# Dilated attention of a two-layer decoder: blocks spread over more steps, negated scores, combinations on two engines, x norms through the weight ring

## The chip, the cores and the metric

The kernel runs on one core of a Trainium2 chip. The metric is the time of one execution on the device in microseconds (us), and lower is better. A core has TensorE (PE; its weight loads are shown as PEld), VectorE (DVE), ScalarE (ACT), GpSimd (POOL) and a queue, SyncE (SP), from which this kernel issues its transfers between DRAM and the on-chip memory (SBUF). Results of matrix products land in PSUM, here eight banks of 128 x 512 words. Each engine works through its own list of instructions in order; semaphores tie the lists together.

## The reference

One sequence of 2048 tokens of width 1024 passes two layers, in float32. Layer 0 is an mLSTM mixer (four heads, a recurrent matrix memory with a running maximum), layer 1 is causal attention with three groups of four heads, which all read the same keys and values. Group `g` sees 128 keys back at a distance of 1, 4 or 16 tokens. After each mixer a gated embedding is added.

```python
def dilated_layer(h, k, v, norm_g, w_in, qnorm_g, w_out, cos, sin):
    proj = rms_norm(h, norm_g) @ w_in
    q, z = jnp.split(proj, [B_QW], axis=-1)
    q = apply_rope(rms_norm(q, qnorm_g), cos, sin)       # 3 groups x 4 heads x 128
    for g, (window, dilation) in enumerate(((128, 1), (512, 4), (2048, 16))):
        o_g, l_g = dilated_window_attention(q[:, :, g], k, v, window, dilation)
        ...
    wts = jax.nn.softmax(jnp.stack(lses, axis=0), axis=0)
    o = jnp.einsum('gbsh,gbshd->bshd', wts, jnp.stack(outs, axis=0))
    return (o.reshape(...) * jax.nn.silu(z)) @ w_out

for layer in range(2):
    h = h + (mlstm_layer(...) if layer == 0 else dilated_layer(...))
    h = h + (p[layer] @ w_ple[layer]) * jax.nn.sigmoid(rms_norm(h) @ w_ple_gate[layer])
```

## The kernel before

**Products.** Tokens are worked in four groups `g` of 512 (four tiles of 128). Each float32 operand is split into a rounded high part and the rest (`wh`, `wl`; `xh`, `xl`), and three products are added in PSUM. `project` (L150) runs a projection: per step of 128 rows of the weights it loads `wraw` on SP, splits it on ScalarE (`wh`, L102) and VectorE (`wl`, L104 or L106), and issues 12 products of 128 x 512 (L167 or L169). `wraw`, `wh` and `wl` are rings of five buffers each. Loads are written with a higher priority, so that the scheduler puts them ahead.

**Side work.** After each step `project` calls `pump()`, which advances the first generator of the list `side` by one step. So the steps of the mLSTM, and later of the attention, are laid between projections. `staged(units)` starts one attention unit per call and advances those that live. A unit (`attend`) is one block of 128 queries: loads `kr`, `qr`, `vt`; transposes to `kT`, `qT` (L664, copies L666); scores (L695); mask and row maximum in one VectorE operation into `pr` and `md` (L701); the negated maximum `nm` (L704); `exp` on ScalarE with the sum (L707); transposes of `pr` (L715, copies L719); products with the values (L726); then `finish`. For groups 1 and 2 `finish` is `spill`: the output on ScalarE (L734) and the statistics on VectorE (L735) go to `ot`, and from there to `o1d` or `o2d` in DRAM (L736). For group 0 it is `combine`: it loads the other two groups' rows to `oo`, forms weights from the three statistics, and adds the three outputs (L776, L778) into `y`, which POOL multiplies with `z` (L780). `held_back` does this later for the four tiles of the first token group. `turn` transposes finished `y` (L182) for the output projection.

**Stages.** For each `g`: `a_in` (projections of layer 0; `norms(g + 1)` reads the next x into `xraw`, L318, and squares it), `a_out` (`mix_out`, then `ple(0, g)`), and `b_in`, which projects keys (`w_kv`), values, queries and `z`. `normrope` normalises and rotates on the way to DRAM: L594 and L600 on VectorE, L601 to L605 on POOL. Its tables `tab` are made on POOL from `cst` (L571, L576 to L578), a load per table. The blocks of group 1 start after `a_out` of the last `g`; group 2 and the rest start in `b_in(3)` after its `queries(2)`. What is left of the list runs afterwards with no products beside it, up to the transposes of `y`; then `mix_out` and `ple` of layer 1 follow for each `g`, with group 0's blocks of the next ones between their steps.

## Time and profile before

| | us |
|---|---|
| median of 3 runs | 2351.04 |
| lowest and highest run | 2348.55, 2352.8 |
| profiled execution, its own time | 2347.66 |
| span of its trace | 2345.8 |
| TensorE busy | 2313.6 |
| VectorE busy | 1543.6 |
| ScalarE busy | 1128.3 |
| POOL busy | 593.0 |

The granted clock of TensorE in the profiled execution is 0.997 of full speed. TensorE's share of the span is 99%; the rows of the engines below it overlap with it and with each other. A row of the waits names the waiting engine, its line and what it waited for; a row of the timeline gives a start, a duration, the engine and line, what is written from what, and in brackets the idle time ahead of it with what ended it.

### The profile page before, as it was taken

How to read it: one execution, taken by the hardware profiler on the slowest of the kernel's cores; microseconds unless marked ns; L12 is line 12 of the kernel's file. 1: busy time of each engine (PE TensorE's matmuls, PEld its weight loads, DVE VectorE, ACT ScalarE, POOL GpSimd, SP SyncE). 2: the span in 40 equal slices, each digit the busy share in tenths (PEclk: the TensorE clock that was granted, in tenths of full speed). 3: DMA queues.
4: the chain of work that ended last, by engine and by line, in shares of the span. 5: the costliest groups of instructions: out<-in, count | busy, mean ns of one | idle time of the engine just before them, and what ended most of it. 6: DMA issues, size and time to landing. Idle time of an engine off the chain costs nothing.

```text
span 2345.8 us, 35374 instructions
## 1 busy us (share of the span) xinstructions
PE 2313.6 (99%) x11760; PEld 1977.5 (84%) x11760; DVE 1543.6 (66%) x3405; ACT 1128.3 (48%) x2731; POOL 593.0 (25%) x719
## 2 busy tenths in 40 slices
PE   9999999999999999999999999999999998999999
PEld 7889888888888888889888888888898887888887
DVE  6846665776566667747575675566755668786866
ACT  5434454543344545434444543344664666453643
POOL 5011235601211644011225601212202121220301
PEclk9999999999999999999999999999999999999999
DMA  5433344533244455333344543253674777465453
GB/s 184 125 91 115 99 149 162 183 116 121 61 123 125 146 164 165 117 91 111 103 130 142 174 125 120 64 171 117 203 221 134 231 237 228 135 198 164 145 160 98
DMA packets 190246, 337.14 MB, mean 144 GB/s; under 512 B 21552, under 2 KB 38256, under 8 KB 190064
## 3 DMA queue, kind: packets, MB, share of 16 engines
q1 hardware_dynamic: 189920, 334.86, 46.1%
q8 instruction: 93, 1.52, 0.3%
q14 instruction: 89, 0.73, 0.1%
q10 hardware_dynamic: 144, 0.02, 0.0%
HBM read 284.27 MB, written 50.53 MB: 143 GB/s over the span
## 4 chain that ended last, share of the span: by engine, by line
PE 85%; DVE 6%; DMA 4%; POOL 2%; ACT 2%; issue 1%; SPq 0%; ACTq 0%; DVEq 0%; POOLq 0%
PE bank L169 41%; PE bank L167 32%; PE bank L726 2%; PE bank L695 2%; PE bank L664 1%; DVE wl L104 1%; PE bank L525 1%; PE bank L526 1%; PE bank L528 1%; PE bank L715 1%; PE bank L182 1%; DMA oo<-o2d 1%; PE bank L512 1%; DMA o2d<-ot 1%; DVE xl L106 1%
## 5 line engine op out<-in xcount | busy, mean ns | idle before, releaser
L169 PE MATMUL bank<-wh,xh 128*128 128x512 f32 (+1 forms) x1664 | 642.5, 386 | 2.8 <-ACT wh L102 2.8
L169 PE MATMUL bank<-wl,xh 128*128 128x512 f32 (+1 forms) x1664 | 622.0, 374 | 0.8 <-DVE wl L104 0.8
L169 PE MATMUL bank<-wh,xl 128*128 128x512 f32 (+1 forms) x1664 | 622.6, 374 | 0.0
L102 ACT ACTIVATE wh<-wraw 128x512 fp32r<-128x512 f32 (+1 forms) x544 | 326.7, 603 | 549.5 <-PE bank L167 302.8
L104 DVE TENSOR_TENSOR wl<-wraw,wh 128x512 fp32r<-128x512 f32 (+1 forms) x512 | 353.9, 695 | 318.7 <-ACT wh L102 317.3
L167 PE MATMUL bank<-xh,wh 128*128 128x512 f32 x1272 | 501.9, 395 | 0.4 <-ACT xh L102 0.4
L167 PE MATMUL bank<-xh,wl 128*128 128x512 f32 x1272 | 496.0, 390 | 0.0
L167 PE MATMUL bank<-xl,wh 128*128 128x512 f32 x1272 | 495.9, 390 | 0.0
L169 PEld LDWEIGHTS bank<-wh,xh 128*128 128x128 f32 x1664 | 313.9, 189 | 51.0 <-ACT wh L102 3.1
L169 PEld LDWEIGHTS bank<-wh,xl 128*128 128x128 f32 x1664 | 313.4, 188 | 50.3
L169 PEld LDWEIGHTS bank<-wl,xh 128*128 128x128 f32 x1664 | 314.2, 189 | 49.3 <-DVE wl L104 1.2
L206 POOL TENSOR_TENSOR acc<-acc,sq 128x512 f32<-128x512 f32 x105 | 162.1, 1545 | 546.7 <-ACT sq L205 543.8
L167 PEld LDWEIGHTS bank<-xl,wh 128*128 128x128 f32 x1272 | 239.1, 188 | 50.5
L167 PEld LDWEIGHTS bank<-xh,wh 128*128 128x128 f32 x1272 | 239.4, 188 | 48.3 <-ACT xh L102 0.6
L167 PEld LDWEIGHTS bank<-xh,wl 128*128 128x128 f32 x1272 | 239.6, 188 | 47.8
L106 DVE SCALAR_TENSOR_TENSOR wl<-wraw,gam,wh 128x512 fp32r<-128x512 f32 x192 | 159.8, 833 | 154.1 <-ACT wh L102 151.5
L102 ACT ACTIVATE wh<-wraw,gam 128x512 fp32r<-128x512 f32 x192 | 138.0, 721 | 195.2 <-PE bank L169 134.8
L707 ACT ACTIVATE pr<-pr,nm 128x256 f32<-128x256 f32 (+1 forms) x192 | 86.6, 453 | 43.5 <-DVE nm L704 43.3
L601 POOL TENSOR_SCALAR ssb<-ssb,r 128x4 f32<-128x4 f32 x64 | 27.3, 426 | 254.1 <-ACT jk L194 233.0
L695 PE MATMUL bank<-kT,qT 128*128 128x128 f32 x600 | 78.5, 278 | 7.0 <-DVE pT L719 2.9
L695 PEld LDWEIGHTS bank<-kT,qT 128*128 128x128 f32 x600 | 72.8, 192 | 10.5 <-DVE pT L719 4.5
L726 PEld LDWEIGHTS bank<-vt,pT 128*128 128x128 f32 x600 | 75.3, 194 | 3.9
(413 smaller groups left out, 2957.4 us busy)
## 6 DMA issues: line engine op xcount, KB each, us to landing
wraw<-in_w_pg SPq DMA_DIRECT2D x128, 256.0 KB, 2.8
wraw<-in_w_in_b SPq DMA_DIRECT2D x128, 256.0 KB, 2.8
wraw<-in_w_z SPq DMA_DIRECT2D x96, 172.0 KB, 2.3
wraw<-in_w_v SPq DMA_DIRECT2D x64, 256.0 KB, 2.6
wraw<-in_w_o SPq DMA_DIRECT2D x64, 256.0 KB, 2.7
wraw<-in_w_out_a SPq DMA_DIRECT2D x64, 256.0 KB, 2.6
wraw<-in_w_kv SPq DMA_DIRECT2D x64, 256.0 KB, 2.7
kr<-kd SPq DMA_DIRECT2D x53, 256.0 KB, 4.2
```

The costliest lines, as they stand in the source:

```text
L102: nc.scalar.mul(dst_h, src, scale)
L104: nc.vector.tensor_tensor(dst_l, src, dst_h.bitcast(F32), op=ALU.subtract)
L106: nc.vector.scalar_tensor_tensor(dst_l, src, scale, dst_h.bitcast(F32), op0=ALU.mult, op1=ALU.subtract)
L167: nc.tensor.matmul(acc[i], w[:, cs], x, start=first, stop=last)
L169: nc.tensor.matmul(acc[i][:, :n], x[:, cs], w, start=first, stop=last)
L182: nc.tensor.transpose(tp[:, t * P:(t + 1) * P], tiles[t][:, k * P:(k + 1) * P], ident)
L206: eng.tensor_tensor(acc, acc, sq, op=ALU.add)
L512: nc.tensor.matmul(sp[:, h * P:(h + 1) * P], qk[:, NH + h, ts_], qk[:, h, ts_], start=True, stop=True)
L601: nc.gpsimd.tensor_scalar(ss, ss, r2[:, t:t + 1], EPS, op0=ALU.mult, op1=ALU.add)
L695: nc.tensor.matmul(sp[:, hh * n + j * P:hh * n + (j + 1) * P], qT[:, hs], kvs[j]["k"][:, hs], start=True, stop=True)
L707: nc.scalar.activation(pr[:, hh, :n], pr[:, hh, :n], AF.Exp, bias=nm[:, h:h + 1], accum_out=md[:, 4 + h:5 + h])
L726: nc.tensor.matmul(op[:, hs], pTs[h // 2][:, c0 + j * P:c0 + (j + 1) * P], kvs[j]["v"][:, hs], start=j == 0, stop=j == nk - 1)
```

## The change

The change has seven parts.

1. `norms(g + 1)`: the loads of x use the ring `wraw`, one per step of the first `w_o` projection, instead of their own `xraw`.
2. Rope tables: four loads `cst` in four buffers serve both tables of a token group (before, one load per table in two buffers). `b_in` projects `queries(2)` first, then keys, values, the other queries and `z`.
3. `normrope`: the addition `ob + tt` moves from VectorE to POOL.
4. `attend`: queries are scaled by a negative number, masks are positive, the row minimum is taken, and `exp` uses a scale of -1 with `md` as its bias, so `nm` is gone. A unit with one key block uses one bank, one `pr` and one `pT` for its four heads. The statistics are written straight into `ot`, which has two buffers.
5. The combination: per tile, two wide POOL multiplications and two wide VectorE additions replace eight small VectorE operations; the two maxima and the sums become reductions. `held_back` loads three steps later.
6. The order of units: the first sixteen (group 1's blocks 0 to 2, group 0's first four) start after `mix_out` of the last `g`, one every two steps (`GAP`); after `queries` of `b_in(3)` come group 2, the combinations of the first tiles, group 0's next four and group 1's last block.
7. `ple(1, 0)`'s 48 products with `w_p` run ahead of layer 1 with attention steps between, and their results are kept (`early`). The unhidden steps `EX` are gone. `WARM` is 20 instead of 24.

```diff
+GAP = 1
-WARM = 24
+WARM = 20
     def norms(g):
-        sq = new_acc()
-        for k in range(KD):
-            raw = wp.tile([P, T], F32, name="xraw", tag="xraw", bufs=2)
-            nc.sync.dma_start(raw, I["xT"][g, k])
-            squares(sq, k, raw)
+        def one(k):
+            with tc.high_priority(offset=PRE // 2):
+                raw = raw_piece(I["xT"][g, k], T)
+                ...
+                squares(sq[0], k, raw)
...
-            acc = project(I["w_o"][grp], 512, 8, X, False)
+            acc = project(I["w_o"][grp], 512, 8, X, False, hooks={} if grp else nsq)
...
-        cst = sm.tile([P, P], F32, name="cst", tag="cst", bufs=2)
+        cst = sm.tile([P, P], F32, name="cst", tag="cst", bufs=NT)
...
-            nc.vector.tensor_tensor(ob, ob, tt, op=ALU.add)
+            nc.gpsimd.tensor_tensor(ob, ob, tt, op=ALU.add)
...
+        queries(2, {5: lambda: st.update(r=token_rstd(sq))})
+        tabk = [rope_table(c, 0) for c in csts]
+        acc = project(I["w_kv"][0], 512, 8, X, False, gam[:, G_KV])
...
-        queries(2)
         late()
         queries(1)
...
                 nc.vector.tensor_tensor_reduce(
-                    out=pr[:, hh, :n], in0=sp[:, hh * n:(hh + 1) * n], in1=mk,
-                    scale=1.0, scalar=-3.0e38, op0=ALU.add, op1=ALU.max, accum_out=md[:, h:h + 1])
-            nc.vector.tensor_scalar_mul(nm[:, h0:h0 + 2], md[:, h0:h0 + 2], -1.0)
...
+                    out=pr[:, cs], in0=sp[:, cs], in1=mk,
+                    scale=1.0, scalar=3.0e38, op0=ALU.add, op1=ALU.min, accum_out=md[:, h:h + 1])
+                nc.scalar.activation(pr[:, cs], pr[:, cs], AF.Exp, scale=-1.0, bias=md[:, h:h + 1],
+                                     accum_out=md[:, 4 + h:5 + h])
...
     def spill(od, r, res, b):
-        def go(op, md):
-            ot = bp.tile([P, 520], F32, name="ot", tag="ot", bufs=1)
-            nc.scalar.copy(ot[:, 0:512], op)
-            nc.vector.tensor_copy(ot[:, 512:], md)
+        def begin():
+            ot = bp.tile([P, 520], F32, name="ot", tag="ot", bufs=2)
+            return ot, ot[:, 0:8]
+        def go(op, ot):
+            nc.scalar.copy(ot[:, 8:520], op)
             nc.sync.dma_start(strided(od, r, res, b, 0, 520), ot)
...
-                nc.scalar.mul(y[:, hs], op[:, hs], ee[:, 0, h:h + 1])
-                for j in range(2):
-                    nc.vector.scalar_tensor_tensor(
-                        y[:, hs], oo[:, j, hs], ee[:, 1 + j, h:h + 1], y[:, hs], op0=ALU.mult, op1=ALU.add)
+        for j in range(2):
+            o3 = oo[:, 520 * j + 8:520 * j + 520].rearrange("p (h c) -> p h c", h=NH)
+            nc.gpsimd.tensor_tensor(o3, o3, ee[:, j].unsqueeze(2).broadcast_to([P, NH, P]), op=ALU.mult)
+        for h in range(NH):
+            nc.scalar.mul(y[:, hs], op[:, hs], ee[:, 2, h:h + 1])
+        for j in range(2):
+            nc.vector.tensor_tensor(y, y, oo[:, 520 * j + 8:520 * j + 520], op=ALU.add)
...
+    def begin():
+        nonlocal bp
+        pa.close()
+        bp = ctx.enter_context(tc.tile_pool(name="bp", bufs=2))
+        side.append(staged(group1(range(3), {}) + group0(0, True), GAP))
+    X, sq = a_out(NG - 1, *a_in(NG - 1), begin)
+    b_in(NG - 1, X, sq, lambda: side.append(staged(
+        group2() + combined(0) + group0(1, False) + group1((3,), {}))))
...
+    early = {}
+    pT = embedded(1, 0)
+    for grp in range(2):
+        acc = project(I["w_p"][1, grp], 512, 2, pT, True, 0.5)
+        early[grp] = [pj() if grp == 0 else bp.tile([P, 512], F32, name="ep", tag="ep", bufs=NT) for _ in acc]
+        ...
+                nc.scalar.copy(e, a)
-    for _ in range(EX):
-        pump()
```

The scheduler sets the order of each engine's list. Three places follow; the line numbers of the changed kernel are its own. The first is SP near the start of the kernel, while group 0's `w_k` and `w_z` are loaded. Before:

```order
L571 DMA cst<-in_cs 128x128 x2
L111 DMA wraw<-in_w_z 128x344
L571 DMA cst<-in_cs 128x128 x2
L111 DMA wraw<-in_w_z 128x344
L318 DMA xraw<-in_xT 128x512 x2
L571 DMA cst<-in_cs 128x128 x2
L111 DMA wraw<-in_w_z 128x344
L318 DMA xraw<-in_xT 128x512 x2
```

And in the changed kernel, at the same place:

```order
L586 DMA cst<-in_cs 128x128
L110 DMA wraw<-in_w_k 128x512 x4
L586 DMA cst<-in_cs 128x128
L110 DMA wraw<-in_w_k 128x512
L586 DMA cst<-in_cs 128x128 x4
L110 DMA wraw<-in_w_k 128x512
L586 DMA cst<-in_cs 128x128 x2
L110 DMA wraw<-in_w_z 128x344 x8
```

The `cst` loads moved ahead of `w_z`, whose eight loads stand together; the `xraw` loads are gone from here.

The second place is ScalarE in the middle of group 2's units, under the projections of `b_in(3)`. Numbers behind a name tell one buffer's use from the next. Before:

```order
L734 COPY ot_18741<-bank_18736 128x512
L719 COPY pT_18753<-bank_18750 128x256
L666 COPY kT_18780<-bank_18775 128x512
L707 ACTIVATE pr_18760,md_18755<-pr_18760,nm_18756 128x128 x2
L707 ACTIVATE pr_18769,md_18755<-pr_18769,nm_18756 128x128 x2
L102 ACTIVATE wh_19270<-wraw_19268,gam_86 128x512
L734 COPY ot_18818<-bank_18813 128x512
```

In the changed kernel `ot_18595`, `ot_18662` and `ot_18729` belong to three units in a row:

```order
L755 COPY ot_18595<-bank_18715 128x512
L689 COPY kT_18749<-bank_18744 128x512
L727 ACTIVATE pr_18735,ot_18729<-pr_18735,ot_18729 128x128 x2
L101 ACTIVATE wh_19185<-wraw_19183,gam_86 128x512
L727 ACTIVATE pr_18735,ot_18729<-pr_18735,ot_18729 128x128 x2
L755 COPY ot_18662<-bank_18782 128x512
```

The output copy of a unit now stands behind the four `exp` of the unit after it, one `pT` copy is gone, and the `exp` write into `ot`.

The third place is TensorE near the end of the attention, in the steps before the first transposes of `y`. Before:

```order
L664 MATMUL bank_20191<-ident_75,kr_20163 128x128 x4
L664 MATMUL bank_20198<-ident_75,qr_20165 128x128 x4
L715 MATMUL bank_20211<-ident_75,pr_20174 128x128 x4
L715 MATMUL bank_20218<-ident_75,pr_20185 128x128 x2
L695 MATMUL bank_20227<-kT_20143,qT_20203 128x128
```

In the changed kernel, where `xh_19622` and `wh_19992` are p and `w_p` of layer 1:

```order
L687 MATMUL bank_19959<-ident_75,kr_19853 128x128 x4
L687 MATMUL bank_19966<-ident_75,qr_19855 128x128 x4
L166 MATMUL bank_19867<-xh_19622,wh_19992 128x512
L687 MATMUL bank_19973<-ident_75,kr_19857 128x128 x4
L166 MATMUL bank_19867<-xh_19622,wl_19993 128x512
```

The products of the embedding, which stood in `ple(1, 0)`, now lie between the transposes of the last units.

More of the change, by code (lines that the diff above doesn't have):

```diff
@@ L33 @@
 W0 = 4
-NL = 2
-EX = 3
+GAP = 1
 HO = {0: (6,), 1: (7, 2), 2: (3,), 3: (4,), 4: (5,)}
@@ L313, in norms, with first @@
     def norms(g):
-        sq = new_acc()
-        for k in range(KD):
-            raw = wp.tile([P, T], F32, name="xraw", tag="xraw", bufs=2)
-            nc.sync.dma_start(raw, I["xT"][g, k])
-            squares(sq, k, raw)
-        ahead[g] = st = {}
-        return rstd_hooks(st, sq, N1, N2, "rba")
+        sq = []
+        def one(k):
+            with tc.high_priority(offset=PRE // 2):
+                raw = raw_piece(I["xT"][g, k], T)
+                if not sq:
+                    sq.append(new_acc())
+                squares(sq[0], k, raw)
+        ahead[g] = st = {}
+        def first():
+            st["r"] = token_rstd(sq[0])
+            st["d"] = spread(st["r"])
+        return {k: lambda k=k: one(k) for k in range(KD)}, {
+            N1: first, N2: lambda: st.update(rb=row_rstd(st["d"], "rba"))}
     def a_in(g):
@@ L605, in normrope @@
             nc.gpsimd.tensor_tensor(o3, o3, rq.unsqueeze(2).broadcast_to([P, NH, P]), op=ALU.mult)
             nc.sync.dma_start(dst, ob)
-        tabk = [rope_table(g, t, 0) for t in range(NT)]
-        st = {}
-        acc = project(I["w_kv"][0], 512, 8, X, False, gam[:, G_KV], hooks={5: lambda: st.update(r=token_rstd(sq))})
-        rst = st["r"]
-        half = sm.tile([P, NT], F32, name="halfb", tag="halfb", bufs=2)
-        nc.vector.tensor_scalar_mul(half, rst, 0.5)
-        r2 = sm.tile([P, NT], F32, name="r2", tag="r2", bufs=2)
@@ L615, in b_in, with queries @@
-        nc.vector.scalar_tensor_tensor(r2, rst, 1.0 / P, rst, op0=ALU.mult, op1=ALU.mult)
+        csts = [angles(g, t) for t in range(NT)]
+        tabs = [rope_table(c, 1) for c in csts]
+        def queries(grp, hooks={}):
+            acc = project(I["w_in_b"][grp], 512, 8, X, False, gam[:, G_B], hooks=hooks)
+            if hooks:
+                settle()
+            with tc.high_priority(offset=EVAC):
+                for t in range(NT):
+                    normrope(acc[t], t, 1, -P ** -0.5, qd[rows(t), grp * 512:(grp + 1) * 512], tabs[t])
@@ L624, in b_in @@
                 nc.sync.dma_start(vd[rows(t), :], b)
-        tabs = [rope_table(g, t, 1) for t in range(NT)]
-        def queries(grp):
-            acc = project(I["w_in_b"][grp], 512, 8, X, False, gam[:, G_B])
-            with tc.high_priority(offset=EVAC):
-                for t in range(NT):
-                    normrope(acc[t], t, 1, P ** -0.5, qd[rows(t), grp * 512:(grp + 1) * 512], tabs[t])
-        queries(2)
         late()
@@ L784, in keep, with combine @@
+    def combine(n):
+        return lambda: stats("md"), lambda op, md: mix(n, *loads(n), op, md)
     def keep(y, held):
@@ L787, in go, with staged @@
             held.append(md)
-        return go
+        return lambda: stats("md0"), go
     def held_back(n, y, held):
-        _, loads, mix = combine(n, y)
-        t = loads()
         yield
-        mix(*t, y, held[0])
         yield
-    def staged(units):
+        yield
+        t = loads(n)
+        yield
+        mix(n, *t, y, held[0], y)
+        yield
+    def staged(units, gap=0):
         live = []
@@ L810, in staged @@
             yield
+            for _ in range(gap):
+                yield
     def group1(blocks, kvs):
@@ L844, in turn @@
         transposed(ys[g], (k,), None, X)
+    early = {}
[3 more added lines that the diff above has]
+        early[grp] = [pj() if grp == 0 else bp.tile([P, 512], F32, name="ep", tag="ep", bufs=NT) for _ in acc]
+        with tc.high_priority(offset=EVAC):
+            for e, a in zip(early[grp], acc):
+                nc.scalar.copy(e, a)
     Y = {}
     while len(done0) < NT:
-        pump()
-    for _ in range(EX):
         pump()
```

165 lines of the change are left out of this document (82 added, 83 removed).

## The prediction

> **What bounds the kernel now.** I read the page first, then the waits of TensorE over the whole trace, then its busy time by stretch, and last the places where it waits.
>
> ```profile
> span 2345.8 us, 35374 instructions
> PE 2313.6 (99%) x11760; PEld 1977.5 (84%) x11760; DVE 1543.6 (66%) x3405; ACT 1128.3 (48%) x2731; POOL 593.0 (25%) x719
> ```
>
> TensorE works for 2313.6 of 2345.8 us. The change keeps all its products but four warm-ups, so it can win only TensorE's 32.2 us of idle time and what hangs on it. It takes 336 instructions from VectorE, which is no gain by itself. The waits say where the idle time is (columns: us in total, times, longest).
>
> ```profile
> PE bank L715 <- ACT pr L707: 4.1, 5, 2.0
> PE bank L664 <- DMA qr<-qd: 3.5, 1, 3.5
> PE bank L695 <- DVE pT L719: 2.9, 3, 1.2
> PE bank L169 <- ACT wh L102: 2.8, 1, 2.8
> PE bank L664 <- DMA kr<-kd: 2.5, 1, 2.5
> PE bank L462 <- DVE ga L452: 1.8, 1, 1.8
> PE bank L695 <- ACT xh L102: 1.7, 1, 1.7
> PE bank L169 <- DVE wl L104: 0.8, 1, 0.8
> 52.00:90.00 38.00, 32.53 (x163) 28.99 (x162) 34.45 (x74) 16.39 (x34) 7.25 (x13) 0.91 0.46 131
> 90.00:1640.00 1550.00, 1549.87 (x7413) 1314.44 (x7412) 990.42 (x1931) 702.39 (x1615) 435.74 (x532) 1.00 0.41 126
> 1805.00:1905.00 100.00, 96.91 (x658) 87.08 (x657) 65.67 (x254) 67.38 (x249) 22.38 (x32) 1.00 0.69 220
> 1926.00:1963.00 37.00, 28.29 (x203) 24.70 (x202) 30.83 (x127) 24.96 (x72) 5.63 (x4) 0.95 0.85 269
> ```
>
> In the windows the first numbers are the stretch and TensorE's busy time, then weight loads, VectorE, ScalarE, POOL, the granted clock, and the DMA share. From 90 to 1640 us TensorE is full: whatever the change does there is worth nothing unless it opens a gap. The idle time stands near the start (5.5 us in 52 to 90) and in the attention from 1640 on.
>
> **The change part by part: the start.** In before, SP stands at the rope-table loads and the `xraw` loads with the `w_z` weights behind them.
>
> ```profile
> SPq L571 <- POOL tab L577: 15.8, 8, 3.1
> 29.17 0.52 POOL L576 TENSOR_TENSOR tab<-qkg,cst 128x64 f32<-128x64 f32 x1 [2.57 <-DMA cst<-in_cs]
> 53.92 0.38 SPq L111 DMA_DIRECT2D wraw<-in_w_z  x1
> 54.51 0.32 PE L169 MATMUL bank<-wl,xh 128*128 128x344 f32 x1
> 54.67 0.32 PE L169 MATMUL bank<-wh,xl 128*128 128x344 f32 x1
> 57.81 0.66 PE L169 MATMUL bank<-wh,xh 128*128 128x344 f32 x1 [2.83 <-ACT wh L102]
> 60.05 0.49 PE L169 MATMUL bank<-wh,xh 128*128 128x344 f32 x1
> 60.34 0.49 PE L169 MATMUL bank<-wl,xh 128*128 128x344 f32 x1
> 1.42 5.38 PE L75 MATMUL bank<-onesr 128*128 128x128 f32 x24 [1.42 <-DVE onesr L64]
> ```
>
> SP waits 15.8 us in eight places for POOL's tables, 2.0 each. A weight goes out at 53.92, and the products that want it could have started at 54.83 and have to wait, 2.8 + 0.8 us. After that products start 0.29 us apart (60.05, 60.34) instead of 0.16 (54.51, 54.67), for some 16 products until about 64 us: another 2.1 us, and the row of 52 to 90 has a granted clock of 0.91. In the changed order four `cst` buffers serve both tables, `xraw` is gone from here, and all eight `w_z` loads stand together before the `w_v` loads. POOL's eight tables, begun at 29.17 and 2.0 us each, then end by about 46 us, and the first `w_z` product is due at about 53. I take the 3.6 and the 2.1 as won, and 1.4 of the 1.8 at `ga`, which waits for VectorE's backlog. If the tables stay in the way, nothing is won. Four warm-ups fewer are worth between 0 and 4 x 0.22 = 0.9 (5.38 / 24 each), since the first product also waits for its weights; I take 0.35. Start: -7.45 (range 0 to -8.7).
>
> **Norms through the weight ring.** 24 loads of x move from the start of `w_z` into the first `w_o` projection, in the ring with the weights. SP carries one load more per step of 12 products (2.7 us at the 0.23 from start to start shown below), and ScalarE one square. The cover is the full stretch 90 to 1640; I cost it at 0. If a slot came back late, each of 24 steps could lose some tenths, at most 5 us in all.
>
> **The first units of attention.** Before, twelve block units start after `w_q` of the last group and wait 1.7 us for `xh`. Now `staged` with a gap of one starts them under the embedding stage, one unit every two steps, 44 steps in all. TensorE has 24 products per unit there. I win 1 us of the old wait and charge 1.5 for attention at three projection changes that had none (0 to 5, the 2.9 us at L695 above being what three such changes cost before). Sum +0.5.
>
> **Queries before keys.** Group 2's first unit reads `qd` just after the store.
>
> ```profile
> 1796.04 0.32 SPq L606 DMA_DIRECT2D qd<-pj  x1
> 1801.13 0.88 PE L664 MATMUL bank<-ident,qr 128*128 128x128 f32 x4 [3.50 <-DMA qr<-qd]
> 1802.66 0.63 PE L169 MATMUL bank<-wh,xl 128*128 128x512 f32 x1
> 1805.24 0.39 PE L169 MATMUL bank<-wh,xh 128*128 128x512 f32 x1
> 1805.47 0.40 PE L169 MATMUL bank<-wl,xh 128*128 128x512 f32 x1
> ```
>
> TensorE waits 3.5 us, then some eight products run 0.63 long until a later one takes 0.39 again, starting 0.23 apart (1805.24, 1805.47): 0.2 more for each, 1.7. Now `queries(2)` comes three projections before its first reader. -5.2 (0 to -5.2; what is late next is `kd`, whose last store lies a projection back).
>
> **Minimum of negated scores, statistics in `ot`.** 96 `nm` operations and 32 `ot<-md` copies leave VectorE; of the 4.1 us that TensorE waited for `pr` I take 0.9 as won (0 to 2), since an `exp` now follows its `ISA` without `nm`. But the first `ISA` of a unit now writes `ot`, which has two buffers, so it waits for the store of the unit two before. That store follows the `ot` copy on ScalarE, which stands behind the four `exp` of the unit between. This closes a loop once per unit. (Units with one key block also copy `pT` once on VectorE, instead of half on each engine; the transposes stay the same, and I cost that at 0, since VectorE is busy 3.15 of 6.00 us in the row of 1864 below.)
>
> ```profile
> 1864.39 0.58 ACT L734 COPY ot<-bank 128x512 f32<-128x512 f32 x1 [0.21 <-PE bank L726]
> 1859.06 0.32 SPq L736 DMA_DIRECT2D o2d<-ot  x1
> 1865.00 0.32 SPq L736 DMA_DIRECT2D o2d<-ot  x1
> 1868.48 0.17 DVE L735 COPY ot<-md 128x8 f32<-128x8 f32 x1 [1.14 <-DMA o2d<-ot]
> 1865.23 0.29 DVE L701 CUSTOM_DVE_ANT_0 pr<-bank,masks 128x128 f32<-128x128 f32 x1
> 1866.70 0.41 ACT L707 ACTIVATE pr<-pr,nm 128x128 f32<-128x128 f32 x1
> 1867.87 0.39 ACT L707 ACTIVATE pr<-pr,nm 128x128 f32<-128x128 f32 x1
> 1869.40 0.72 ACT L102 ACTIVATE wh<-wraw,gam 128x512 fp32r<-128x512 f32 x1 [1.05 <-PE bank L169]
> 1864.00:1870.00 6.00, 6.00 (x43) 5.49 (x43) 3.15 (x14) 3.77 (x13) 0.00 (x0) 1.00 0.70 224
> DMA to landing us min/median/max: 2.5/3.0/5.3
> ```
>
> Before, a unit takes 5.94 us (issue to issue, 1859.06 to 1865.00) with TensorE full. The new loop: `ISA` to `exp` 0.37, four `exp` 1.56 (1866.70 to 1868.26), one `wh` between them 0.72, the copy 0.58, the issue 0.03, the store. The store's landing is 3.0 in the median, and 3.5 in the unit shown (1865.00 to 1868.48); I take 3.3, since units come without a pause. Sum 6.56, and 0.1 less for overlapping operations on ScalarE: 6.46, or 0.52 more than before. With 15 units in the stretch that is +7.8. With a landing of 2.5 the loop is 5.7 and costs nothing; with 5.3 it is 8.5, +38. While VectorE stands, `wl` and `qT` stand behind it, so TensorE has no way round. The Trainium skill, DMA: Bandwidth & Descriptors (Anatomy of one DMA), fits a transfer as about 2.0 us plus its bytes at 436 GB/s, 2.6 us for these 260 KB (estimate); by that the loop is 5.8 us and the 7.8 fall away. The row's median of 3.0 is longer than the page's number. The stretch's old stalls at projection changes (3.1 us in 1805 to 1905) mostly stay: -1.1. The group 2 stretch: +6.7 (-4 to +38).
>
> **Wide combinations and the tail.** Per token tile, eight `stt` on VectorE become two multiplications on POOL and two additions.
>
> ```profile
> L605 POOL TENSOR_TENSOR pj<-pj,rq 128x512 f32<-128x512 f32 x64 | 71.0, 1110 | 5.1
> L206 POOL TENSOR_TENSOR acc<-acc,sq 128x512 f32<-128x512 f32 x105 | 162.1, 1545 | 546.7 <-ACT sq L205 543.8
> ```
>
> A multiplication costs POOL 1.11 to 1.55 us, so a combination of 8 x 0.35 on VectorE becomes 2.2 to 3.1 on POOL and 1.4 on VectorE, one after the other: not shorter, but on an idle engine. In before, the end of attention (1926 to 1963) runs with few products: 8.7 us idle, and about 1.5 more at half clock. Now each step there has 12 products of layer 1's embedding beside it, and these leave `ple(1,0)`; their eight evictions on ScalarE (0.58 each, as the `ot` copy) I cost at 0, beside products. VectorE still stands at the combination's first operation, which needs a store and a load in a row (3.0 each at least), and TensorE at the last `y`. I leave 5.5 of the 10.2: -4.7 (range -9 to +5). The 64 `ob` additions of `normrope` on POOL (1.1 to 1.55 each, four per projection of 21.8 us) make four rows of about 5.1 us there, 20 of 21.8: hidden while TensorE is the bound. If POOL fell behind, the eight `pj` buffers would hold VectorE and then the banks.
>
> **The sum.** -7.45 + 0.5 - 5.2 - 0.9 + 6.7 - 4.7 = -11.05. The profiled execution took 2347.66 us, so 2336.6; the median of the runs, 2351.04, is 3.4 above it, so 2340.
>
> **The rivals.** The first: the store lands within 2.5 to 2.8 us, the loop stays under 5.94, and 7.8 more are won: 2332. For it speaks that the median of 3.0 includes a busy queue; against it, the waits of 3.5. The Trainium skill's fit above would give this result.
>
> The second is that an expected gain is not there: the tables still hold `w_z` (+7.45), or the tail keeps its stalls and adds POOL's multiplications to the chain (+4.7, or more). Then 2345 to 2348, within the 0.2% (4.7 us) that a measurement here can tell from no change. For the tail speaks that VectorE was busy 30.8 of 37 us there. The Trainium skill, SBUF — State Buffer (Who interferes with whom), adds that a VectorE instruction with two inputs in SBUF and a POOL instruction that reads SBUF exclude each other; eight multiplications of 1.11 us (the row of L605) would then stop VectorE for up to 8.9 us in the tail, and the 4.7 would be gone (estimate). Before has no wide POOL operation that reads `oo` there, so no run here shows it yet.
>
> The third ends slower: the loop's store lands later than 4.35 us in most units. The loop is then over 7.5 us, 15 units cost over 23.5, more than everything won (-18.85 without the loop) and 4.7 besides: 2356 and up. The maximum of 5.3 speaks for it, and that the stretch's DMA share is 0.69 already; against it, the median.
>
> **How the numbers follow.** The forecast's case 0.45 (2336 to 2346), the hidden loop 0.26, a gain that fails 0.17, the slow loop 0.12. Of the forecast's case 0.05 lies within 0.2%. So faster 0.66, same 0.22, slower 0.12. The range 2329 to 2355 leaves out the ends of the first and third rival.
>
> **What would show it.** Right: no gap at 54 us and eight `w_z` issues in a row before 50; no wait of TensorE for `qr`; a wait of VectorE's `ISA` for `o2d<-ot` in each unit of group 2, and some 6.5 us between `o2d` issues; waits of TensorE for `pr`, `pT` or `wl` of about 0.5 us in each. Wrong: issues still 5.94 apart; gaps in 90 to 1640, from the x loads in the ring or POOL behind in `normrope`; or a tail with more than 5.5 us idle.

## The result, and the profile after

The changed kernel takes 2405.28 us in the median of four runs (2401.86 to 2406.36), the kernel before 2350.31 beside it. The ratio is 1.0231, with a 95% interval of 1.0213 to 1.0248: slower by 55 us. The forecast was 2340, with a range of 2329 to 2355. The first rows are from the page of the changed kernel, then its waits of TensorE over the whole trace, and three windows:

```profile
span 2403.0 us, 35091 instructions
PE 2337.9 (97%) x11756; PEld 1986.5 (83%) x11756; DVE 1521.0 (63%) x3069; ACT 1125.6 (47%) x2718; POOL 692.2 (29%) x815
...
PE bank L166 <- ACT wh L101: 18.2, 3, 6.2
PE bank L734 <- ACT pr L727: 15.8, 14, 4.5
...
PE bank L504 <- ACT rw__5514 L495: 2.3, 1, 2.3
...
52.00:90.00 38.00, 38.00 (x209) 33.86 (x208) 30.79 (x73) 16.62 (x32) 2.55 (x6) 1.00 0.43 130
90.00:1640.00 1550.00, 1520.36 (x7213) 1285.72 (x7212) 957.82 (x1839) 688.31 (x1592) 481.28 (x581) 0.99 0.40 124
...
1626.00:2403.00 777.00, 742.98 (x4187) 636.18 (x4185) 504.89 (x1104) 401.31 (x1063) 191.35 (x173) 0.99 0.54 170
```

The gap at the start is gone (38.00 of 38.00 us), and so is the wait for `qr`. But the stretch from 90 to 1640 us, which was full, now has 29.6 us without products: three waits of about 6 us for `wh`, and a few of about 2 us in the mLSTM. From the last embedding stage of layer 0 to the end, the changed kernel needs 777 us; the kernel before needed this:

```profile
1590.90:2346.00 755.10, 729.74 (x4187) 632.14 (x4185) 520.56 (x1392) 404.27 (x1076) 137.19 (x125) 0.99 0.56 176
```

TensorE's busy time there also grew, by 13.2 us for the same products. Part of that is the clock. In the clock records of the two traces this stretch has 20.5 us at half clock, and 8.6 before, which makes about 6 of the 13.2 us (estimate); where the rest comes from is open. Over the whole run the mean granted clock fell from 0.997 to 0.989, which is worth some 19 of the 57 us between the two spans (0.011 x 2403 less 0.003 x 2346, an estimate).

Most of what follows is read from one table. It gives the us from the first product of a stage to the first of the next, taken from the start times of the products in each trace (stages with no difference left out; the last row is the rest of the span, with the fourth `b_in` in it).

| stage | before | changed | addition on VectorE | three `ot` | both |
|---|---|---|---|---|---|
| start to v of the first group | 74.3 | 67.8 | 67.0 | 68.0 | 66.8 |
| v and w_o, first group | 104.7 | 108.1 | 108.0 | 108.8 | 107.9 |
| v and w_o, second | 102.8 | 110.3 | 109.6 | 110.4 | 108.7 |
| v and w_o, third | 102.8 | 108.9 | 108.1 | 108.8 | 108.7 |
| b_in, first group | 131.5 | 137.4 | 131.5 | 136.4 | 131.5 |
| b_in, second | 131.5 | 137.9 | 131.5 | 137.3 | 131.5 |
| b_in, third | 131.5 | 137.8 | 131.5 | 137.8 | 131.5 |
| w_q and w_k, groups two to four | 130.6 | 136.6 | 130.8 | 139.4 | 131.1 |
| ple(0,3) to the end | 755.0 | 777.0 | 766.6 | 757.0 | 753.9 |

### The profile page after: what moved, and what is told of

Read it like the earlier page. It is cut to its first block, busy times and chain, and to the rows that moved or that the text cites. A ratio compares the mean times of both kernels' runs of the same rounds, so it can differ in the third digit from the quotient of the medians.

```text
span 2403.0 us, 35091 instructions
## 1 busy us (share of the span) xinstructions
PE 2337.9 (97%) x11756; PEld 1986.5 (83%) x11756; DVE 1521.0 (63%) x3069; ACT 1125.6 (47%) x2718; POOL 692.2 (29%) x815
## 5 line engine op out<-in xcount | busy, mean ns | idle before, releaser
L103 DVE TENSOR_TENSOR wl<-wraw,wh 128x512 fp32r<-128x512 f32 (+1 forms) x512 | 364.3, 716 | 307.1 <-ACT wh L101 302.7
L166 PE MATMUL bank<-xh,wh 128*128 128x512 f32 x1272 | 506.4, 398 | 18.9 <-ACT wh L101 18.2
L105 DVE SCALAR_TENSOR_TENSOR wl<-wraw,gam,wh 128x512 fp32r<-128x512 f32 x192 | 175.3, 918 | 174.9 <-ACT wh L101 174.1
L166 PEld LDWEIGHTS bank<-xh,wl 128*128 128x128 f32 x1272 | 241.1, 190 | 49.5 <-DVE wl L103 1.6
L101 ACT ACTIVATE wh<-wraw,gam 128x512 fp32r<-128x512 f32 x192 | 137.0, 719 | 204.5 <-PE bank L168 107.5
L619 POOL TENSOR_TENSOR pj<-pj 128x512 f32<-128x512 f32 x64 | 85.5, 1337 | 200.9 <-DVE pj L613 199.8
L724 DVE CUSTOM_DVE_ANT_0 pr<-bank,masks 128x256 f32<-128x256 f32 (+1 forms) x192 | 60.8, 361 | 57.9 <-DMA o2d<-ot 26.2
L727 ACT ACTIVATE pr<-pr,ot 128x128 f32<-128x128 f32 (+1 forms) x128 | 55.1, 432 | 74.0 <-DVE ot L724 73.9
L188 POOL TENSOR_TENSOR rr<-rsq,mhalf 128x2 f32<-128x2 f32 x32 | 24.0, 751 | 209.3 <-DVE rsq L187 209.3
```

The lines of the kernel that those rows point to most:

```text
L101: nc.scalar.mul(dst_h, src, scale)
L103: nc.vector.tensor_tensor(dst_l, src, dst_h.bitcast(F32), op=ALU.subtract)
L105: nc.vector.scalar_tensor_tensor(dst_l, src, scale, dst_h.bitcast(F32), op0=ALU.mult, op1=ALU.subtract)
L166: nc.tensor.matmul(acc[i], w[:, cs], x, start=first, stop=last)
L619: nc.gpsimd.tensor_tensor(ob, ob, tt, op=ALU.add)
L724: nc.vector.tensor_tensor_reduce(out=pr[:, cs], in0=sp[:, cs], in1=mk, scale=1.0, scalar=3.0e38, op0=ALU.add, op1=ALU.min, accum_out=md[:, ...
```

## The experiments

Each ratio is against the kernel before, run beside it on the same chip. A difference from another kernel is one of medians, mostly from different chips; taken from the ratios they come out up to 2 us off.

### The addition of normrope

The first runs change one thing in the changed kernel, or bring one part alone into the kernel before.

```diff
-            nc.gpsimd.tensor_tensor(ob, ob, tt, op=ALU.add)
+            nc.vector.tensor_tensor(ob, ob, tt, op=ALU.add)
```

> The changed kernel with one edit: the addition ob + tt of normrope is back on VectorE. Theory A (POOL's longer normrope chain makes the qd stores late, and on SP the next group's x and w_q loads stand behind those stores): the three gaps of 5.8 to 6.2 us before w_q go, b_in(0) to b_in(2) take 131.5 to 133 us each instead of 137.4 to 137.9, and w_q, w_k 43.5 instead of 45.3 to 45.9, so about -25 there; in b_in(3) the o2d stores no longer wait behind qd, some -3 to -6 more: 2374 to 2380. Rival B (the rope tables made in between, or the new order of the projections, hold SP): the gaps stay above 5 us, 2400 or more.

Measured: 2368.51 us, ratio 1.0081 (1.0066 to 1.0096). That is 36.8 less than the changed kernel (35.3 by the ratios). b_in is back at 131.5 for all three groups. It was more than theory A expected, since `b_in(3)` also got 12.0 shorter (265.4 to 253.3). The other way round, the same single line moved to POOL in the kernel before:

> The kernel before with one edit: the addition ob + tt on POOL. Theory A (that alone pushes POOL over the time of a projection and SP with it): b_in(0) to b_in(2) 5 to 7 us longer and w_q, w_k 2 longer, +20 to +27: 2370 to 2377. Rival B (it needs the new order of projections and tables): 2349 to 2354.

Measured: 2401.18 us, ratio 1.0223 (1.0200 to 1.0247), 51 us for one line. Theory A had the kind right and half the size: in this trace b_in is 7 to 13 us longer in the three groups, w_q and w_k are 9.2 longer in all, and from ple(0,3) on it is 21 longer, which the theory did not have. Rival B falls, as the order of projections is not needed. The trace of the changed kernel shows the way at the end of `b_in(0)`:

```profile
SPq L625 <- POOL pj L624: 8.9, 3, 6.0
SPq L586 <- POOL tab L596: 5.1, 1, 5.1
...
452.01 1.03 POOL L624 TENSOR_TENSOR pj<-pj,rq 128x512 f32<-128x512 f32 x1
453.07 0.33 SPq L625 DMA_DIRECT2D qd<-pj  x1
453.49 1.10 SPq L110 DMA_DIRECT2D wraw<-in_xT  x2
456.59 0.72 ACT L101 ACTIVATE xh<-wraw,gam 128x512 fp32r<-128x512 f32 x1 [5.12 <-DMA wraw<-in_xT]
456.94 2.52 SPq L110 DMA_DIRECT2D wraw<-in_w_q  x4
461.20 0.79 PE L166 MATMUL bank<-xh,wh 128*128 128x512 f32 x1 [5.80 <-ACT wh L101]
417.60:461.20 43.60, 37.80 (x167) 30.97 (x165) 21.64 (x35) 19.77 (x64) 38.06 (x54) 0.96 0.46 149
```

SP waits for POOL before it may issue a store of queries (453.07, after POOL's 452.01) and a `cst` load. The loads of the next group's x and `w_q` stand behind these. The last of x went out after 456 and `w_q` from 456.94 on; the products before had ended at 455.4, and TensorE stood for 5.80 us. After that the products start 0.43 us apart (462.52 and 462.95) instead of 0.23, which is the longer w_q and w_k in the table. The last row is the window of the last 43.6 us of `b_in(0)` (its columns as in the prediction): POOL is busy for 38.06. The same stretch in the kernel before, and with the addition on VectorE:

```profile
414.80:458.40 43.60, 43.60 (x194) 36.10 (x193) 30.85 (x51) 24.23 (x81) 32.44 (x48) 1.00 0.51 161
```
```profile
410.70:454.30 43.60, 43.60 (x195) 36.07 (x193) 30.34 (x50) 24.57 (x82) 32.10 (x48) 1.00 0.49 162
```

SP's waits for POOL are not new. Its wait for the last operation of `normrope`, over most of `b_in(0)` (340 to 460 us before, 330 to 462 in the changed kernel):

```profile
SPq L606 <- POOL pj L605: 38.3, 13, 4.1
```
```profile
SPq L625 <- POOL pj L624: 39.0, 11, 6.0
```

What differs is the lead of the loads. The first `w_q` load goes out at 452.95 in the kernel before and at 448.86 with the addition on VectorE, 5.4 us before the products of `b_in(0)` end in both; in the changed kernel it goes out 1.5 us after their end:

```profile
452.95 1.74 SPq L111 DMA_DIRECT2D wraw<-in_w_q  x3
```
```profile
448.86 1.89 SPq L110 DMA_DIRECT2D wraw<-in_w_q  x3
```

Is SP's order the whole way, or does POOL's backlog hold TensorE by itself? Two runs take POOL's results off SP, with the addition still on POOL.

```diff
-            nc.sync.dma_start(dst, ob)
+            nc.gpsimd.dma_start(dst, ob)
```

> The changed kernel, the addition still on POOL, with the stores of keys and queries issued by POOL instead of SP. Theory A (the delay passes through SP's order: loads stand behind a store that waits for POOL): the three gaps before w_q go although POOL works as long as before, b_in 131.5 to 133 each, -20 to -30: 2375 to 2385. Rival B (POOL itself is behind and holds pj tiles, VectorE and the banks): b_in stays 137 or longer, 2400 or more; POOL's own issue time may add to it.

Measured: 2393.25 us, ratio 1.0179 (1.0164 to 1.0195). b_in takes 137.0, 136.0 and 131.5. This run does not tell the theories apart: on SP the `cst` loads still wait for POOL. So these moved as well:

```diff
-        nc.sync.dma_start(cst, I["cs"][n * P:(n + 1) * P, :])
+        nc.gpsimd.dma_start(cst, I["cs"][n * P:(n + 1) * P, :])
```

> The changed kernel with the stores of keys and queries and the loads of cst on POOL's queue, so that nothing on SP in b_in waits for POOL. Theory A (the delay passes through SP's order; the run with the stores alone failed since the cst loads on SP wait for POOL too): b_in(0) to b_in(2) 131.5 to 133, w_q, w_k 43.5 to 44.5, 2370 to 2385. Rival B (POOL's backlog holds pj tiles and banks): b_in 136 and more, 2390 and more.

Measured: 2404.57 us, ratio 1.0233 (1.0217 to 1.0248). b_in is 131.5 in all three groups, as theory A said, but w_q and w_k now take 53.0, 52.2 and 50.3 instead of 43.5, and the time misses theory A's range. Nothing is won. ScalarE's rows and the wait of TensorE in the second group's w_q:

```profile
PE bank L166 <- ACT wh L101: 6.5, 1, 6.5
...
471.09 0.69 ACT L666 ACTIVATE pj<-bank,halfb 128x512 f32<-128x512 f32 x1 [5.86 <-POOL rq L622]
483.08 0.69 ACT L667 ACTIVATE pj<-bank,halfb 128x512 f32<-128x512 f32 x1 [7.17 <-DMA qd<-pj]
```

ScalarE's evictions of `z` need `pj` tiles that POOL's chain still holds, and the next `wh` stand behind them. SP's order is the first way, and when it is opened the backlog comes out at the `pj` ring. But POOL's own issues of these transfers (0.6 us each) add to its backlog in these two runs, so how far the `pj` ring would hold TensorE without them is not shown. Is the addition alone too much, or only with the next group's rope tables in the same stretch? The tables go to VectorE, the addition stays on POOL:

```diff
-            nc.gpsimd.tensor_tensor(tab[:, 0, a], q[:, a], c, op=ALU.mult)
+            nc.vector.tensor_tensor(tab[:, 0, a], q[:, a], c, op=ALU.mult)
```
(and the other two operations of `rope_table` likewise)

> The changed kernel, the addition still on POOL, with the rope tables made on VectorE. Theory A (POOL falls behind since the next group's tables, some 16 to 18 us of its work, stand between the normrope chains of the last two query projections; the addition alone would fit): the gaps before w_q go, b_in 131.5 to 133: 2374 to 2382. Rival B (five POOL operations per tile are too long by themselves): b_in 135 or longer, 2390 or more.

Measured: 2391.59 us, ratio 1.0174 (1.0158 to 1.0189), 13.7 less than the changed kernel. b_in is 133.1, 133.9 and 134.5:

```profile
PE bank L166 <- ACT wh L101: 6.6, 3, 2.9
```

The three waits fall from 18.2 to 6.6 us, so for them the tables are the larger part, as theory A has it. But w_q and w_k and the stages from ple(0,3) on stay as long as in the changed kernel (138.9 and 776.8), and the time lies in rival B's range (b_in lies between the two). Of the 36.8 us of the addition the tables make 13.7; the chain with five operations is too long by itself. In this trace two of its rounds of four tiles take POOL 19.3 and 22.2 us (412.24 to 431.55, 434.47 to 456.71), and a projection takes 21.8.

### The norms through the weight ring

> The kernel before with part 1 alone: x for the norms through the weight ring. Theory A (ScalarE stands at squares whose x is late, with the mLSTM's exp behind them, and the ring has fewer weights ahead): the stages of v and w_o take 2 to 4.6 and 1.3 to 3 us longer for three groups as in the changed kernel, +17 in all, and the start wins 2 to 5 since no xraw stands there: 2362 to 2366 against 2350. Rival B (the longer v and w_o come from the late start of the group after b_in, by other parts): v and w_o as before, 2346 to 2350.

Measured: 2357.89 us, ratio 1.0036 (1.0024 to 1.0049). The start to v takes 68.5 (74.3 before), then v and w_o take 108.0, 109.9 and 108.4 against 104.7, 102.8 and 102.8: +16.1 and -5.8. The stages do what theory A says; the time lies below its range, as the start won more and attention was 3.4 shorter in this trace. It also shows that most of the start's gain (5.8 of some 7.5) comes from the missing `xraw` loads, since this run leaves the `cst` buffers alone. The changed kernel in the second group's v:

```profile
558.69 0.63 ACT L204 ACTIVATE sq<-wraw 128x512 f32<-128x512 f32 x1 [3.52 <-DMA wraw<-in_xT]
563.60 1.40 POOL L205 TENSOR_TENSOR acc<-acc,sq 128x512 f32<-128x512 f32 x1 [2.75 <-ACT sq L204]
563.80 1.47 DVE L487 TENSOR_TENSOR_SCAN rows<-ones,mcar,ra__5513 4x128 f32<-4x128 f32 x1
565.62 0.31 ACT L489 ACTIVATE rows<-rows 4x128 f32<-4x128 f32 x1 [2.16 <-DVE rows L488]
566.17 0.22 PE L504 MATMUL bank<-ident,rw__5514 4*128 4x4 f32 x1 [2.27 <-ACT rw__5514 L495]
```

ScalarE stands at a square of x (3.52 us), and what the mLSTM needs of it comes after. In v and w_o of this group TensorE waits for results of ScalarE for the mLSTM and for `v`, 5.0 us in all, and never for `wh`. One of these waits (2.27 us) also has VectorE's scan in its chain, 1.47 us here and 0.47 in the kernel before. With the addition on VectorE and three `ot` buffers as a base (2355.76 us, next section), four runs change where x goes and when it is squared:

```diff
-                raw = raw_piece(I["xT"][g, k], T)
+                raw = pj()
+                nc.sync.dma_start(raw, I["xT"][g, k])
```

> As the run with the addition on VectorE and three ot buffers, and x for the norms loaded into pj tiles instead of the weight ring, same hooks and priorities. Theory A (the ring is too short for weights and x together): v and w_o fall from 53.7 and 54.4 to 56 to 49.8 and 53, -13 to -15. Rival B (ScalarE stands at a square whose x has just been issued, with the mLSTM's operations behind it): v and w_o stay as they are, within 3 us in all.

Measured: 2356.46 us. w_o is at 53.0 in all groups, but v takes 54.9, 55.5 and 55.9: the convolution needs the same `pj` tiles, and TensorE waits 10.6 us for `ga` in all. In the next run the square is written one step after its load:

```diff
-                squares(sq[0], k, raw)
...
+            if k:
+                two(k - 1)
...
```
(`two(k - 1)` writes the square of the step before)

> As the run with x in pj tiles, and each square is written one step after its load, at normal priority. Theory A (ring alone): no more than 2 us from the run with pj tiles. Rival B (late x in front of the mLSTM's operations on ScalarE): v and w_o at 49.8 to 51 and 53, -10 to -15 against the run with the ring.

Measured: 2355.06 us, w_o 53.0, v 56.1, 56.1 and 53.0. Delaying the square does not help here, so rival B finds no support in these tiles; with x in the ring a later square was not tried. Then buffers of its own, first at the same steps, then as in the kernel before:

```diff
+                raw = ap.tile([P, T], F32, name="xraw", tag="xraw", bufs=3)
+                nc.sync.dma_start(raw, I["xT"][g, k])
```

> As the run with the addition on VectorE and three ot buffers (2355.8), and x for the norms in three buffers of its own, at the same steps of w_o and with the same priority. Theory A (x takes places of the weight ring or, in the run with pj tiles, of the convolution's tiles): v and w_o return to 49.8 (51.7 in the first group) and 53, -14 to -17 in all: 2339 to 2343. Rival B (loads and squares at these steps are themselves in the way, whatever the buffer): v and w_o stay 4 to 6 longer for three groups, 2353 to 2357.

> As before, and the norms written as in the kernel before the change: two xraw buffers of their own, no steps, so the loads come early. Theory A: v and w_o at 49.8 and 53, as in the kernel before; the start keeps its gain if the four cst buffers alone made it (z2 at 14.7: 2337 to 2341), and loses it if the xraw loads held w_z too (z2 at 21: 2344 to 2348).

Measured: 2350.95 us, ratio 1.0005 (0.9994 to 1.0017), and 2349.70 us, ratio 0.9994 (0.9985 to 1.0004). In groups two and three, v and w_o are at 49.7 to 49.8 and 53.0 in both, as theory A said: the same loads and squares cost nothing when x has tiles that nothing else needs. But the start to v is 76.3 and 76.0 again: loads of x with free buffers go out early, between the first `w_k` and `w_z`. With four `cst` buffers and `xraw` as before, the start has no gain at all. The two wishes exclude each other in the first group only.

### The loop through `ot`

```diff
-            ot = bp.tile([P, 520], F32, name="ot", tag="ot", bufs=2)
+            ot = bp.tile([P, 520], F32, name="ot", tag="ot", bufs=3)
-        zt = bp.tile([P, 512], F32, name="zt", tag="zt", bufs=2)
+        zt = bp.tile([P, 512], F32, name="zt", tag="zt", bufs=1)
```

> The changed kernel with three ot buffers instead of two (and one zt buffer to make room). Theory A (the loop of ISA, exp, copy, store and landing sets the pace of group 2, as predicted): the spacing of o2d issues falls from 6.8 to about 6.0, the waits of ISA for o2d (26 us) go, and the stretch gets some 10 to 14 us shorter: 2391 to 2396. Rival B (what holds it is the o2d issue behind the qd stores on SP, and TensorE's own work): under 4 us, 2401 or more.

Measured: 2388.38 us, ratio 1.0160 (1.0145 to 1.0175), 16.9 less than the changed kernel; more than theory A expected. The `o2d` issues are 5.85 us apart in the median, and 6.91 in the changed kernel. One unit of group 2 in the changed kernel:

```profile
1877.69 0.57 ACT L755 COPY ot<-bank 128x512 f32<-128x512 f32 x1
1881.57 0.32 SPq L625 DMA_DIRECT2D qd<-pj  x1
1882.96 0.38 SPq L756 DMA_DIRECT2D o2d<-ot  x1
1886.77 0.29 DVE L724 CUSTOM_DVE_ANT_0 pr<-bank,masks 128x128 f32<-128x128 f32 x1 [5.66 <-DMA o2d<-ot]
1887.65 0.40 PE L734 MATMUL bank<-ident,pr 128*128 128x128 f32 x1 [4.54 <-ACT pr L727]
```

The output is copied at 1878.3, but SP issues its store only at 1882.96, behind a `qd` store that waited for POOL. VectorE's first operation on the scores stands for 5.66 us, and TensorE 4.54. So the two causes meet in this stretch. Both edits together:

> The changed kernel with the addition on VectorE and three ot buffers (one zt). If the two causes are separate, their gains of 37 and 17 us add: about 2352; if they share the stores' queue on SP (qd stores that delay o2d issues), the sum is smaller by 4 to 8: 2356 to 2360. Left over then against the kernel before: the norms in the ring, 8 to 15 us, less the gains at the start and at qr.

Measured: 2355.76 us, ratio 1.0022 (1.0012 to 1.0031). Separate gains of 36.8 and 16.9 would give 2351.6: 4.2 us are shared (2.9 by the ratios), hardly more than the medians can tell. Without POOL's backlog the second edit is worth 2368.51 - 2355.76 = 12.7. One unit of group 2 with the addition on VectorE and two `ot` buffers:

```profile
1876.89 0.36 SPq L756 DMA_DIRECT2D o2d<-ot  x1
1880.80 0.29 DVE L724 CUSTOM_DVE_ANT_0 pr<-bank,masks 128x128 f32<-128x128 f32 x1 [2.19 <-DMA o2d<-ot]
1883.89 0.36 SPq L756 DMA_DIRECT2D o2d<-ot  x1
```

VectorE's first operation on the next scores follows the issue of the store that it waits for by 3.9 us, and the next issue is 7.0 us after the first. In the median of the 13 waits it is 3.3 us, and the issues are 6.56 apart in the median of all units, 5.85 with three buffers. The second edit also hides a loss. From ple(0,3) to the second token group of layer 1 it wins 18.1 us (477.4 to 459.3), and from there to the end it loses 5.4 (289.2 to 294.6). `ot` is no longer used there, but `zt` is, with one buffer instead of two. All kernels here with two `zt` buffers take 288.7 to 290.6 us for this stretch, and all with one `zt` and three `ot` take 294.2 to 298.0. SP's wait for POOL ahead of the loads of `zt` grows from 3.8 to 15.2 us; the kernel before, with one `zt` buffer too, waits as long (15.9) and takes 289.3, so what makes the loss is not shown. VectorE's wait for `o2d` in the changed kernel, with the addition on VectorE, and with three `ot` buffers too:

```profile
DVE pr L724 <- DMA o2d<-ot: 26.2, 11, 5.7
```
```profile
DVE pr L724 <- DMA o2d<-ot: 18.3, 13, 4.5
```
```profile
DVE pr L724 <- DMA o2d<-ot: 0.3, 1, 0.3
```

### The rest of attention

The combination back on VectorE, on the base of 2355.76:

```diff
-            nc.gpsimd.tensor_tensor(o3, o3, ee[:, j].unsqueeze(2).broadcast_to([P, NH, P]), op=ALU.mult)
...
-            nc.vector.tensor_tensor(y, y, oo[:, 520 * j + 8:520 * j + 520], op=ALU.add)
+                nc.vector.scalar_tensor_tensor(
+                    y[:, hs], oo[:, 520 * j + 8 + h * P:520 * j + 136 + h * P], ee[:, j, h:h + 1], y[:, hs],
+                    op0=ALU.mult, op1=ALU.add)
```

> As the run with the addition on VectorE and three ot buffers (2355.8), with the combination's eight small operations on VectorE instead of two on POOL and two on VectorE. If POOL's multiplications were only moved work beside TensorE: within 2 us. If they lengthen the chain to the last y (POOL then VectorE) or stop VectorE, -3 to -6. If they do what was hoped for: +3 to +6.

Measured: 2356.68 us, 0.9 more than its base: no difference that can be told. The next kernel puts together what the runs pointed to:

```diff
     def norms(g):
+        if g > 1:
...
+                raw = ap.tile([P, T], F32, name="xraw", tag="xraw", bufs=2)
```
(the third and fourth group's x in buffers of its own, loaded early; the second group's stays in the ring; and the addition on VectorE, three `ot` buffers, one `zt`)

> The changed kernel with the addition on VectorE, three ot buffers, and x for the norms through the weight ring for the second token group alone (so that the start stays free of x loads), through two buffers of its own for the third and fourth. Theory (the start wins about 8, v and w_o lose about 3 once instead of three times, attention is 1 to 2 shorter than in the kernel before): 2341 to 2345, so 6 to 9 below the kernel before. If the early x loads of the third group hold w_z again, 2347 to 2350.

Measured: 2343.73 us, ratio 0.9973 (0.9962 to 0.9983): faster than both kernels, by some 6 us against the one before. From its page and its waits of TensorE:

```profile
span 2339.9 us, 35143 instructions
PE 2311.5 (99%) x11756; PEld 1973.3 (84%) x11756; DVE 1539.0 (66%) x3133; ACT 1128.6 (48%) x2718; POOL 638.3 (27%) x751
...
PE bank L743 <- ACT pr L736: 3.2, 3, 2.5
PE bank L727 <- DVE pT L746: 2.9, 3, 1.5
PE bank L727 <- ACT y L806: 2.4, 1, 2.4
```

On this base three parts were undone one at a time. First the products moved ahead of `ple(1, 0)`:

```diff
-    pT = embedded(1, 0)
-    for grp in range(2):
-        acc = project(I["w_p"][1, grp], 512, 2, pT, True, 0.5)
-        ...
+    early = {}
```

> As the first of this call, with ple(1,0)'s products with w_p back in ple(1,0), so the end of attention runs with few products beside it. As predicted for the tail (4.7 us won by the products beside it): 3 to 7 slower than the first. Rival (the end waits for the combination's chain in any case, and the eight kept results cost as much): within 2.

Measured: 2356.98 us, ratio 1.0033 (1.0021 to 1.0046), 13.3 more than its base. By the traces 3.8 us lie in layer 0, which the edit does not touch, and from ple(0,3) on it is 767.7 against 753.2; the trace is of the slowest of the five runs. So the products beside are worth some 10 to 14. The longest wait there, and the same wait in the kernel before:

```profile
PE bank L181 <- POOL y L809: 8.2, 2, 5.2
```
```profile
PE bank L182 <- POOL y L780: 1.2, 1, 1.2
```

When no products lie beside it, the new end of attention waits longer for `y` than the old one. POOL's multiplications in the chain are a likely reason, but the order of units and the later loads of `held_back` are new as well, and no run takes these apart here. Then the order of the projections, keys and values first:

```diff
-        queries(2, {5: lambda: st.update(r=token_rstd(sq))})
...
+        tabs = [rope_table(c, 1) for c in csts]
+        queries(2)
         late()
```

> As the best kernel so far (addition on VectorE, three ot buffers, x through the ring for one group; 2343.7), with keys and values projected before queries(2) as in the kernel before. As forecast: TensorE waits for qr again for about 3.5 us and runs some eight products at half clock, +5.2: 2347 to 2350. Rival (the first unit of group 2 is late by something else, VectorE's normrope or the banks, in either order): within 2.

Measured: 2351.41 us, ratio 1.0015 (1.0003 to 1.0026) where its base has 0.9973: 0.0042 of 2350, so some 10 us (7.7 between the medians, which are of different chips). That is more than forecast, and the rival falls. The old wait is back, longer:

```profile
PE bank L698 <- DMA qr<-qd: 5.4, 1, 5.4
```

And last the spread of the first sixteen units:

```diff
-GAP = 1
+GAP = 0
```

> As the best kernel so far, with GAP 0: the first sixteen units start one per step instead of one every two steps, so they end early and later steps of ple(0,3) and b_in(3) carry none. As forecast (+0.5 for the spread part, most of the work hidden either way): within 3. Rival (two steps per unit is what keeps ScalarE and VectorE ahead of TensorE in the embedding stage): +5 to +15.

Measured: 2341.53 us, ratio 0.9967 (0.9956 to 0.9979). The intervals overlap with the base's 0.9973 (0.9962 to 0.9983): the spread is worth nothing that can be told, and the rival falls.

## Why the prediction was wrong

The forecast was -10, the result +55. Point by point, by its own terms:

| step | forecast, us | measured, us | from |
|---|---|---|---|
| start | -7.45 | -7.6 | start to v, 74.3 to 66.8 with both edits |
| norms in the ring | 0 (to +5) | +15.1 | v and w_o of three groups, 325.3 against 310.3; alone in the kernel before +16.1 |
| first units spread | +0.5 | +1.4 (-2 to +5) | GAP 1 against 0, by ratio |
| queries first | -5.2 | some -8 to -10 | order undone |
| loop through `ot` | +7.8 | +12.7 (+18.1 up to layer 1) | two against three buffers |
| combination and tail | -4.7 | see below | |
| addition on POOL | 0 | +36.8 | undone in the changed kernel |

**The step that failed most** is the sentence on `normrope`: "four rows of about 5.1 us there, 20 of 21.8: hidden while TensorE is the bound". It put the addition at nothing; it cost 36.8 us. The sentence set POOL's time for one projection against that projection, and three things are wrong with it. The rows leave no slack: with nothing else on POOL, two rounds took 19.3 and 22.2 us, and with the addition on POOL and the tables off it the kernel is still 23 us slower than with the addition on VectorE. POOL also makes the next group's rope tables in the same stretch, which the prediction itself had priced at 2.0 us each: two rounds and the four tables that the trace has in the last 43.6 us of `b_in(0)` come to 48 us by its own prices. These tables make 13.7 of the 36.8. And POOL's results release stores on SP, behind which the next group's loads stand. The prediction named the `pj` buffers as the place where it would show; in the changed kernel it was SP's queue. The kernel before already showed how near this was: in the same window its POOL was busy for 32.44 of 43.60 us, and between 340 and 460 us its SP waited 38.3 us for it.

**The norms** were costed at 0 with at most 5. The bound came from lost tenths per step; what happened is that x came late in the ring that it shares with the weights, ScalarE stood at its square, and TensorE then waited for the mLSTM's results behind it. The cover named, a full TensorE from 90 to 1640, is no cover when the moved work stands in front of what keeps it full.

**The loop** was found and had the right sign, and its spacing was right: the prediction took 3.3 us for the store and 6.46 from issue to issue, and the run with the addition on VectorE has 3.3 and 6.56. The term was under-sized all the same, 18.1 for 7.8 before the loss in layer 1. Without the loop the units are 5.85 us apart and not 5.94, and the prediction counted only the stretch of group 2. By the stages 9.8 of the 18.1 us lie in the last three projections of `b_in(3)`, where group 2's units run, 1.5 in the first three, and the other 6.8 behind them, where the trace with two buffers has two waits of 8.4 us in all for `o1d`, in group 1's last block. Under the embedding stage such waits (6.2 us of VectorE) cost nothing: it takes 90.1 us with two buffers and with three. In the changed kernel the loop was made worse by the `qd` stores ahead of `o2d` on SP. The rival that the store lands early enough falls: with two buffers the 18.3 us of waits are there. The fit of the Trainium skill, DMA: Bandwidth & Descriptors (Anatomy of one DMA), gave estimates of 2.6 us for the store and 5.8 for the loop, and this trace does not agree with them. The Trainium skill states that fit for transfers that GpSimd issues, and SP issues these.

**The start and the queries** came out as forecast or better in time. The start's gain is mostly the missing `xraw` loads, though, and not the `cst` buffers. The first units moved under the embedding stage were not moved back, so of that term only the spread is measured. (In the kernel before they begin after `a_out` of the last group, not after `w_q` as the prediction has it.)

**Combination and tail.** Moving the combination to POOL is neutral while products lie beside it (0.9), and those products are worth some 10 to 14 us in the changed scheme, more than the 4.7 forecast. Both together are not what was summed: repaired, attention from ple(0,3) to the end takes 753.2 against 755.0, where the terms without the loop came to -11.4 (+0.5 - 5.2 - 0.9 - 1.1 - 4.7). Up to the second token group of layer 1 the repaired kernel wins 8.1 us (457.6 against 465.7), and from there on it loses 6.3 (295.6 against 289.3), in stages that the prediction did not list. That is the loss seen above with one `zt` and three `ot` buffers. New short waits have taken the place of the old ones (for `pr`, `pT` and `y`, rows of the repaired kernel above). Which part makes each of these was not taken apart.

The two edits together give 49.5 us (36.8 + 12.7). By the stages of the run with both, what is left against the kernel before is +15.1 - 7.6 - 1.1 = 6.4. That makes 55.9, against 55.0 measured. What the first and the third term share is in the 36.8.

## What to carry to other kernels

Before work is moved to an engine that seems idle, add up all it does in that stretch, the next stage's preparations too, and look at which queue waits for its results: here loads stood on SP behind stores that waited for POOL, and so a helper engine's delay became TensorE's. Compare by how much the first load of the next stage leads the end of this one. A load that shares a ring with the weights is not free, even under a full engine. A buffer written earlier than before (statistics at the start of a unit instead of its end) is held longer by the whole unit, and here it needed one more to keep the pace. What is taken away elsewhere to make room for it has to be measured too.

## What the runs showed of the hardware that was not expected

In the kernel before, all 16 of the running-maximum scans on VectorE (L472, 4x128, inputs in SBUF) take 0.47 us, and none runs beside a POOL instruction. In the changed kernel (L487) 6 of 16 take 1.47 to 1.59. These six, and only these, overlap a POOL addition of two 128x512 tiles, and each ends some 0.28 us after it; the one shown above (563.80) begins 0.2 us after an addition of 1.40 us. With x in its own early buffers all 16 are at 0.47 again. The rule of the Trainium skill, SBUF — State Buffer (Who interferes with whom), that a VectorE instruction with two inputs in SBUF and a POOL instruction that reads SBUF exclude each other, fits this.

The half clock after long waits of TensorE adds to the waits themselves. After the wait of 5.80 us above, w_q and w_k take 45.3 us instead of 43.5.
